# Forgetting attention by pairs of heads with the values as the stationary operand; the mLSTM output gates projected last

## The chip, the cores and the metric

One core of one Trainium2 chip runs the whole program. The metric is the device time of one execution in microseconds (us), and a kernel's time is the median over its runs. The engines are called as in the profile: PE is TensorE's matmuls and PEld its weight loads, DVE is VectorE, ACT is ScalarE, POOL is GpSimd, SP is the queue that issues most DMAs.

## What is computed

Two transformer blocks on 512 tokens of width 1024. The change touches only the mixer of the second block. There 16 meta tokens are put ahead of the 512 (528 rows in all), and two mixers run on the same normalized input: an mLSTM with 4 heads of 128, and a forgetting attention with 8 heads of 64. Cut to what matters:

```python
# mLSTM, per head: h is the stabilised chunk recurrence
h = _rmsnorm(h, out_gain)
h = h * jax.nn.sigmoid(o_pre)
# forgetting attention, per block of 128 queries
logits = einsum('bhtd,bhsd->bhts', qh[:, :, start:end], kh[:, :, :end]) * scale
logits = logits + c[:, :, start:end, None] - c[:, :, None, :end]
logits = where(mask, logits, -inf)
p = softmax(logits)
outs.append(einsum('bhts,bhsd->bhtd', p, vh[:, :, :end]))
# both halves side by side through one output matrix
h_res = h_res + concatenate([y_m, y_f]) @ w_out
```

`o_pre` is a projection of the input (512 columns), `c` the running sum of the forget gates. Later the block ends with a product-key expert layer, which the change leaves alone.

## The kernel before, in words

The program runs through stages: a (gated delta net), b (windowed attention), m (this mixer), p (expert layer). All large projections are made of three fp32r matmuls each (`mm3`, L315 to L317: high by high, high by low, low by high part), accumulated in a PSUM tile `pj`, of which there are two. Weight panels come by `Feed` (line 368): DMA into `wraw`, cast to `whi` on ACT (L233), remainder `wlo` on POOL (L235); six panels are held, in the fixed order of the list that `stage_m` (line 929) hands it, and a panel's place is free when the last step that uses it is done.

In stage m the joint stretch begins where `stage_m` opens the pools `smb` and `pm` (line 1006). Two lists of small steps are built there, each step with a weight, and `weave` (line 334) sorts them into one order by their cumulative weights, so that both lists advance evenly. Within that, a scheduler of the language orders each engine's instructions; an engine then takes them strictly in that order.

- The list `cell` is the mLSTM: first the output-gate projection (16 steps; tanh of it goes into `so`, L1007), then head by head the query and key projections with a convolution (`proj`, taps on DVE in L1195), the weights `mS` (L1216 to L1224, product `pS` on PE), the outputs `pn` (L1232) and, at a head's last tile, the multiplication of the gate and of the norm into `so` (L1246, L1247). Head h+1's projections lie between head h's weights and outputs. For the last head nothing lies there. Then come `mix_turn` (transposes of `so` by PE, `ptz`, L1052) and the first half of the output projection (`mix_out`).
- The list `attend` is the forgetting attention (`fox`): 8 heads, each with 4 query tiles, 32 in all. A tile has three steps. `products`: decay row minus column on DVE (L1281), mask on POOL (L1282), the logits on PE in two matmuls, one for the 16 meta keys (`fo`, L1286) and one for the rest (`pl`, L1287), their minimum with the sum on DVE (L1288, L1289), exponent on ACT (L1290). `turn`: transposes of the probabilities (L1295, L1297) and copies into `fPT`. `values`: one matmul per key tile, with the transposed probabilities as stationary operand (128 columns) and 64 columns of `FV` moving (L1305). At a head's end DVE scales by the reciprocal sums into `yf` (L1308). Before the second half of `mix_out`, `yf` is transposed by PE too.

An ordinary fp32 matmul shows in the trace as two MATMUL and two LDWEIGHTS records; a transpose and an fp32r matmul show as one.

## Time and profile before

| | |
|---|---|
| time, median of 3 runs | 2846.97 us (2841.19 to 2852.54) |
| the profiled execution's own time | 2848.16 us |
| its span, first to last instruction | 2846.4 us |
| mean granted TensorE clock | 0.978 of full |
| PE busy | 2718.2 us (95%) |
| DVE busy | 1973.7 us (69%) |
| ACT busy | 1126.0 us (40%) |
| POOL busy | 836.2 us (29%) |
| the joint stretch of stage m | from about 1235 us to 1484 us, then 23 us of output projection |

How to read it: PE is close to always busy, but busy time counts overlapping matmuls and says nothing of how fast each one went. The clock column (PEclk) tells which of its two levels, 1.2 and 2.4 GHz, PE was granted: 1.00 is 2.4 GHz all through a window, 0.50 is 1.2 GHz all through. The chain of waits says what released each piece of work that the end depended on.

### The profile page before, as it was taken

How to read it: one execution, taken by the hardware profiler on the slowest of the kernel's cores; microseconds unless marked ns; L12 is line 12 of the kernel's file. 1: busy time of each engine (PE TensorE's matmuls, PEld its weight loads, DVE VectorE, ACT ScalarE, POOL GpSimd, SP SyncE). 2: the span in 40 equal slices, each digit the busy share in tenths (PEclk: the TensorE clock that was granted, in tenths of full speed). 3: DMA queues.
4: the chain of work that ended last, by engine and by line, in shares of the span. 5: the costliest groups of instructions: out<-in, count | busy, mean ns of one | idle time of the engine just before them, and what ended most of it. 6: DMA issues, size and time to landing. Idle time of an engine off the chain costs nothing.

```text
span 2846.4 us, 39369 instructions
## 1 busy us (share of the span) xinstructions
PE 2718.2 (95%) x14291; PEld 2250.7 (79%) x14291; DVE 1973.7 (69%) x4339; ACT 1126.0 (40%) x2300; POOL 836.2 (29%) x609
## 2 busy tenths in 40 slices
PE   7999999989999999899998979999999999999999
PEld 5777777767676777677777879899888888888887
DVE  6566666665565645726646899996777877878787
ACT  5444444444444433334322245564333333333332
POOL 0100000000111132232102237774444444444441
PEclk9999999999999999999889989999999999999999
DMA  4112121111222122221103234557999899998996
GB/s 149 53 52 60 60 60 60 53 60 60 75 60 75 62 66 61 63 60 45 31 23 112 87 119 176 177 197 271 308 326 331 316 334 324 318 317 317 319 326 236
DMA packets 170462, 440.92 MB, mean 155 GB/s; under 512 B 13932, under 2 KB 79756, under 8 KB 168604
## 3 DMA queue, kind: packets, MB, share of 16 engines
q1 hardware_dynamic: 133404, 304.17, 33.0%
q0 software_dynamic: 36864, 134.23, 12.5%
q8 instruction: 113, 1.85, 0.3%
q14 instruction: 81, 0.66, 0.1%
HBM read 401.60 MB, written 36.75 MB: 154 GB/s over the span
## 4 chain that ended last, share of the span: by engine, by line
PE 66%; DVE 16%; issue 7%; ACT 5%; DMA 3%; POOL 3%; SPq 0%; ACTq 0%; DVEq 0%; POOLq 0%
PE pj L315 11%; PE pj L316 11%; PE pj L317 10%; PE acc L316 4%; PE acc L317 4%; PE acc L315 3%; PE pG L1611 2%; ACT whio L233 2%; DVE x L1479 2%; DMA raw<-in_v_dram 2%; PE po L922 1%; DVE wloo L235 1%; PE fo L1305 1%; PE po L316 1%; PE po L315 1%
## 5 line engine op out<-in xcount | busy, mean ns | idle before, releaser
L315 PE MATMUL pj<-hThi,whi 128*128 128x384 f32 (+2 forms) x1664 | 603.4, 363 | 2.7 <-ACT hg L1357 2.1
L317 PE MATMUL pj<-hThi,wlo 128*128 128x384 f32 (+2 forms) x1664 | 593.5, 357 | 10.9 <-DVE wlo L235 10.9
L316 PE MATMUL pj<-hTlo,whi 128*128 128x384 f32 (+2 forms) x1664 | 597.4, 359 | 0.2 <-DVE hTlo L213 0.2
L317 PEld LDWEIGHTS pj<-hThi,wlo 128*128 128x128 f32 x1664 | 316.6, 190 | 32.1 <-DVE wlo L235 11.5
L315 PEld LDWEIGHTS pj<-hThi,whi 128*128 128x128 f32 x1664 | 317.1, 191 | 31.1 <-ACT hg L1357 2.7
L316 PEld LDWEIGHTS pj<-hTlo,whi 128*128 128x128 f32 x1664 | 316.8, 190 | 24.8 <-DVE hTlo L213 1.2
L316 PE MATMUL acc<-wloo,Wh 128*128 128x512 f32 x768 | 303.1, 395 | 5.8 <-DVE wloo L235 4.4
L315 PE MATMUL acc<-whio,Wh 128*128 128x512 f32 x768 | 301.2, 392 | 0.8 <-ACT whio L233 0.8
L317 PE MATMUL acc<-whio,Wl 128*128 128x512 f32 x768 | 300.2, 391 | 0.0
L1470 POOL DMA_INDIRECT raw<-in_v_dram,ids x128 | 191.7, 1498 | 238.1 <-DVE wloo L235 120.9
L1470 POOL DMA_INDIRECT raw<-in_u_dram,ids x128 | 185.9, 1452 | 242.6 <-DVE wloo L235 110.9
L212 ACT CAST Wh<-W 128x384 fp32r<-128x384 f32 x128 | 65.7, 513 | 372.9 <-DVE W L1417 337.7
L235 DVE TENSOR_TENSOR wlo<-raw,whi 128x1024 fp32r<-128x1024 f32 x128 | 161.7, 1263 | 71.7 <-ACT whi L233 71.6
L233 ACT CAST whi<-raw 128x1024 fp32r<-128x1024 f32 x144 | 150.2, 1043 | 124.2 <-issue 92.7
L235 DVE TENSOR_TENSOR wloo<-raw,whio 128x1024 fp32r<-128x1024 f32 x128 | 156.9, 1226 | 53.7 <-ACT whio L233 53.7
L316 PEld LDWEIGHTS acc<-wloo,Wh 128*128 128x128 f32 x768 | 144.2, 188 | 46.1 <-DVE wloo L235 18.5
L235 POOL TENSOR_TENSOR wlo<-wraw,whi 128x1024 fp32r<-128x1024 f32 x52 | 124.4, 2406 | 187.3 <-ACT whi L233 187.1
L317 PEld LDWEIGHTS acc<-whio,Wl 128*128 128x128 f32 x768 | 144.2, 188 | 30.5
L315 PEld LDWEIGHTS acc<-whio,Wh 128*128 128x128 f32 x768 | 144.1, 188 | 30.4 <-ACT whio L233 2.4
L1479 DVE SCALAR_TENSOR_TENSOR x<-raw,act,x 128x1024 f32<-128x1024 f32 x128 | 163.8, 1280 | 1.0
L1474 DVE SCALAR_TENSOR_TENSOR raw<-raw,xt 128x1024 f32<-128x1024 f32 x128 | 154.0, 1219 | 0.0
L233 ACT CAST whi<-wraw 128x1024 fp32r<-128x1024 f32 x100 | 104.4, 1047 | 107.0 <-PE pj L316 68.3
(418 smaller groups left out, 5483.4 us busy)
## 6 DMA issues: line engine op xcount, KB each, us to landing
raw<-in_uT_dram SPq DMA_DIRECT2D x128, 512.0 KB, 4.6
raw<-in_v_dram SPq DMA_DIRECT2D x128, 512.0 KB, 5.1
wraw<-in_wa_dram SPq DMA_DIRECT2D x48, 512.0 KB, 3.6
G<-stage SPq DMA_DIRECT2D x12, 2048.0 KB
Gt<-G SPq DMA_DIRECT2D x32, 768.0 KB, 10.3
wraw<-in_wb_dram SPq DMA_DIRECT2D x32, 512.0 KB, 3.8
wraw<-in_wmt_dram SPq DMA_DIRECT2D x20, 512.0 KB, 3.6
H<-hg SPq DMA_DIRECT2D x48, 192.0 KB, 1.9
```

The lines of the kernel that those rows point to most:

```text
L212: self.nc.scalar.copy(hi, src)
L233: nc.scalar.copy(hi, raw)
L235: eng.tensor_tensor(out=lo, in0=raw, in1=hi.bitcast(F32), op=ALU.subtract)
L315: nc.tensor.matmul(out, wh, mh, start=first, stop=False)
L316: nc.tensor.matmul(out, wh, ml, start=False, stop=False)
L317: nc.tensor.matmul(out, wl, mh, start=False, stop=last)
L922: nc.tensor.matmul(po[:, (4 * b + h) * 64 : (4 * b + h + 1) * 64], PT[:, h * nst + st, :], V[:, s0 // P + st, g * 64 : (g + 1) * 64], star ...
L1305: nc.tensor.matmul(d["o"][:, 64 * t : 64 * t + 64], u["PT"][0:n, j, :], FV[0:n, j, h * 64 : (h + 1) * 64], start=(j == 0), stop=(j == t + 1))
L1470: nc.gpsimd.indirect_dma_start(out=g, out_offset=None, in_=src, in_offset=bass.IndirectOffsetOnAxis(ap=ids[:, j : j + 1], axis=0))
L1474: nc.vector.scalar_tensor_tensor(g, g, 1.0, xt0, op0=ALU.mult, op1=ALU.mult, accum_out=act[:, j : j + 1])
L1479: nc.vector.scalar_tensor_tensor(k.x[:, 0, :], g, act[:, j : j + 1], k.x[:, 0, :], op0=ALU.mult, op1=ALU.add)
L1611: nc.tensor.matmul(p[:, n * P : (n + 1) * P], o1[:, n, :], o0[:, n, :], start=True, stop=True)
```

## The change

The attention goes by pairs of heads. A query tile of a pair is one unit (16 in all): both heads' `products`, both heads' `turn`, and one `values`, in which the 64 columns of `FV` are the stationary operand and the transposed probabilities (128 columns) move; head 0 of the pair writes PSUM partitions 0 to 63, head 1 partitions 64 to 127, alternating key tile by key tile. The result is already transposed, so `mix_turn` for `yf` is replaced by `mix_split`, which makes the high and low parts without PE. The division by the sums now runs along partitions: eight matmuls per pair (`pr`) spread the reciprocal sums over the array, ACT copies them, DVE multiplies. The 16 meta keys have no matmul of their own any more for the first three tiles (one product of 144, 272 or 400 columns); only the last, with 528 columns, keeps two. `fo` has one buffer in place of two, and a bank `fm` takes the small pieces.

The output gates of the mLSTM are projected last: eight of the sixteen steps lie between the weights and outputs of head 3, where nothing lay; the other eight follow head 3. `so` holds the normalized outputs first, and `use_gate` multiplies (1 + tanh) in. The first two gate tiles stay in the two `pj` buffers until head 3 is done. The four gate panels move in the feed from ahead of the eight query/key panels to behind them. (V1 is also padded from 130 to 132 columns; the matmul still reads 130.)

```diff
@@ -929,11 +929,11 @@
-    feed = Feed(k, [(a["wmt"][4 * i + c], None) for i in (4, 3, 2, 0, 1) for c in range(4)] + [(a["wmc"][i], None) for i in range(8)]
-                + [(a["wmo"][4 * c + 2 * h + j], None) for h in range(2) for c in range(2) for j in range(2)], 6)
+    feed = Feed(k, [(a["wmt"][4 * i + c], None) for i in (4, 3, 2, 0) for c in range(4)] + [(a["wmc"][i], None) for i in range(8)]
+                + [(a["wmt"][4 + c], None) for c in range(4)] + [(a["wmo"][4 * c + 2 * h + j], None) for h in range(2) for c in range(2) for j in range(2)], 6)
-        yf = s3.tile([P, NT, 512], F32, name="yf")
+        yf = s3.tile([P, 4, T], F32, name="yf")
...
@@ -1004,13 +1004,22 @@
-                cell = tproj(4, range(1, 5), lambda j, n, p: nc.scalar.activation(so[:, j - 1, :], p, AF.Tanh, scale=0.5))
+                held = []
+
+                def use_gate(j, p):
+
+                    th = s2.tile([P, T], F32, tag="mM", name="th")
+                    nc.scalar.activation(th, p, AF.Tanh, scale=0.5)
+                    nc.vector.scalar_tensor_tensor(so[:, j - 1, :], th, 1.0, so[:, j - 1, :], op0=ALU.add, op1=ALU.mult)
+
+                gate = tproj(6, range(1, 5), lambda j, n, p: held.append(p) if j < 3 else use_gate(j, p))
                 heads = [mlstm(k, s2, h, hh, hl, V1, colR, rowM, so, feed) for h in range(4)]
-                cell += heads[0][0][0] + heads[0][0][1]
+                cell = heads[0][0][0] + heads[0][0][1]
                 for h in range(4):
                     (p0, p1), run, w, o = heads[h]
-                    n0, n1 = heads[h + 1][0] if h < 3 else ([], [])
+                    n0, n1 = heads[h + 1][0] if h < 3 else (gate[0:4], gate[4:8])
                     cell += [run] + n0 + w[0:2] + n1 + [w[2], o[0], w[3], o[1], w[4], o[2], o[3]]
+                cell += [(0.1, lambda j=j: use_gate(j, held[j - 1])) for j in (1, 2)] + gate[8:]
...
@@ -1020,21 +1029,22 @@
-                heads = [fox(k, s2, h, fqT, fkT, FV, colC, rowC, yf) for h in range(8)]
-                tiles = [t for _, l in heads for t in l]
-                turns = mix_turn(k, yf, 4, out)
-                attend.append(heads[0][0])
-                for i, (pr, tr, mu) in enumerate(tiles):
+                pairs = [fox(k, s2, c, fqT, fkT, FV, colC, rowC, yf) for c in range(4)]
+                units = [u for _, l in pairs for u in l]
+                turns = mix_split(k, yf, 4, out)
+                attend += pairs[0][0]
+                for i, (pr, tr, _) in enumerate(units):
+                    for j in range(2):
+                        if i:
+                            attend.append(units[i - 1][1][j])
+                        attend.append(pr[j])
+                        if i % 4 == 3 and i < 15:
+                            attend.append(pairs[i // 4 + 1][0][j])
                     if i:
-                        attend.append(tiles[i - 1][1])
-                    attend.append(pr)
-                    if i:
-                        attend.append(tiles[i - 1][2])
-                    if i % 4 == 2 and i // 4 < 7:
-                        attend.append(heads[i // 4 + 1][0])
-                    if i in (28, 29, 30):
-                        attend.append(turns[i - 28])
-                attend += tiles[-1][1:]
+                        attend.append(units[i - 1][2])
+                    if i in (13, 14, 15):
+                        attend.append(turns[i - 13])
+                attend += units[-1][1] + [units[-1][2]]
...
+
+def mix_split(k, y, k0, out):
+
+    def step(kt):
+        yh, yl = out()
+        k.split(yh[:, kt, 0:T], yl[:, kt, 0:T], y[:, kt - k0, :])
+
+    return [(0.1, lambda kt=kt: step(kt)) for kt in range(k0, k0 + 4)]
...
     def proj(j):
-        ct, i0 = 4 * j + h, 20 + 2 * h + j
+        ct, i0 = 4 * j + h, 16 + 2 * h + j
...
@@ -1243,74 +1262,88 @@
         if t == NT - 1:
             r = k.rnorm(d["ss"], 128.0, NT)
             sh = so[:, :, h * P : (h + 1) * P]
-            nc.vector.scalar_tensor_tensor(sh, sh, 1.0, y, op0=ALU.add, op1=ALU.mult)
-            nc.vector.tensor_tensor(out=sh, in0=sh, in1=r.rearrange("p (n o) -> p n o", o=1).to_broadcast([P, NT, P]), op=ALU.mult)
+            nc.vector.tensor_tensor(out=sh, in0=y, in1=r.rearrange("p (n o) -> p n o", o=1).to_broadcast([P, NT, P]), op=ALU.mult)
...
-def fox(k, s2, h, fqT, fkT, FV, colC, C, yf):
-    ct, js = h // 2, slice(64 * (h % 2), 64 * (h % 2) + 64)
     d = {}
+    half = [slice(0, 64), slice(64, P)]
+
+    def gates(j):
...
     def parts(t):
-        u = {}
-
-        def products():
-            if t == 0:
-
-                d["o"] = k.pm.tile([P, 512], F32, tag="fo", name="fo", bufs=2)
-                d["sum"] = k.sm.tile([P, NT], F32, tag="fsm", name="fsm")
-            dB = s2.tile([P, TM], F32, tag="dB", name="dB", bufs=3)
...
+        lg, PT = {}, {}
+        ts = slice(t * P, (t + 1) * P)
+
+        def products(j):
+            h, js = 2 * c + j, half[j]
+            if t == j == 0:
+
+                d["o"] = k.pm.tile([P, 512], F32, tag="fo", name="fo", bufs=1)
+                d["m"] = k.pm.tile([P, 512], F32, tag="fm", name="fm", bufs=1)
+                d["sum"] = k.sm.tile([P, 2, NT], F32, tag="fsm", name="fsm")
+            lg[j] = dB = s2.tile([P, TM], F32, tag="dB", name="dB", bufs=3)
...
-            m = k.sm.tile([P, 2], F32, tag="fm", name="fm")
+            m = k.sm.tile([P, 2], F32, tag="fmm", name="fmm")
             p = ps("pl")
-            qt = fqT[js, ct, t * P : (t + 1) * P]
-            nc.tensor.matmul(pm, qt, fkT[js, ct, 0:16], start=True, stop=True)
-            nc.tensor.matmul(p[:, 0 : W - 16], qt, fkT[js, ct, 16:W], start=True, stop=True)
-            nc.vector.tensor_tensor_reduce(dB[:, 0:16], pm, dB[:, 0:16], 1.0, -NEG, ALU.add, ALU.min, m[:, 0:1])
-            nc.vector.tensor_tensor_reduce(dB[:, 16:W], p[:, 0 : W - 16], dB[:, 16:W], 1.0, m[:, 0:1], ALU.add, ALU.min, m[:, 1:2])
-            nc.scalar.activation(dB[:, 0:W], dB[:, 0:W], AF.Exp, scale=-1.0, bias=m[:, 1:2], accum_out=d["sum"][:, t : t + 1])
-            u["lg"] = dB
-
-        def turn():
-            pt, pmT, lg = ps("pt"), d["o"][0:16, 320:448], u["lg"]
-            nc.tensor.transpose(pmT, lg[:, 0:16], k.ident)
-            for j in range(t + 1):
-                nc.tensor.transpose(pt[:, j * P : (j + 1) * P], lg[:, 16 + j * P : 16 + (j + 1) * P], k.ident)
-            u["PT"] = PT = s2.tile([P, 5, P], F32, tag="fPT", name="fPT", bufs=2)
-            nc.scalar.copy(PT[0:16, 0, :], pmT)
-            nc.vector.tensor_copy(PT[:, 1 : t + 2, :], pt[:, 0 : (t + 1) * P].rearrange("p (j c) -> p j c", c=P))
+            qt = fqT[js, c, ts]
+            if W > 512:
+                pm = d["m"][:, 16 * j : 16 * j + 16]
+                nc.tensor.matmul(pm, qt, fkT[js, c, 0:16], start=True, stop=True)
+                nc.tensor.matmul(p[:, 0 : W - 16], qt, fkT[js, c, 16:W], start=True, stop=True)
+                nc.vector.tensor_tensor_reduce(dB[:, 0:16], pm, dB[:, 0:16], 1.0, -NEG, ALU.add, ALU.min, m[:, 0:1])
+                nc.vector.tensor_tensor_reduce(dB[:, 16:W], p[:, 0 : W - 16], dB[:, 16:W], 1.0, m[:, 0:1], ALU.add, ALU.min, m[:, 1:2])
+            else:
+                nc.tensor.matmul(p[:, 0:W], qt, fkT[js, c, 0:W], start=True, stop=True)
+                nc.vector.tensor_tensor_reduce(dB[:, 0:W], p[:, 0:W], dB[:, 0:W], 1.0, -NEG, ALU.add, ALU.min, m[:, 1:2])
+            nc.scalar.activation(dB[:, 0:W], dB[:, 0:W], AF.Exp, scale=-1.0, bias=m[:, 1:2], accum_out=d["sum"][:, j, t : t + 1])
+
+        def turn(j):
+            pt, o = ps("pt"), 128 + P * ((2 * t + j) % 3)
+            pmT = d["m"][0:16, o : o + P]
+            nc.tensor.transpose(pmT, lg[j][:, 0:16], k.ident)
+            for i in range(t + 1):
+                nc.tensor.transpose(pt[:, i * P : (i + 1) * P], lg[j][:, 16 + i * P : 16 + (i + 1) * P], k.ident)
+            PT[j] = s2.tile([P, 5, P], F32, tag="fPT", name="fPT", bufs=2)
+            nc.scalar.copy(PT[j][0:16, 0, :], pmT)
+            nc.vector.tensor_copy(PT[j][:, 1 : t + 2, :], pt[:, 0 : (t + 1) * P].rearrange("p (j c) -> p j c", c=P))
...
         def values():
-            for j in range(t + 2):
-                n = ST[j][1]
-                nc.tensor.matmul(d["o"][:, 64 * t : 64 * t + 64], u["PT"][0:n, j, :], FV[0:n, j, h * 64 : (h + 1) * 64], start=(j == 0), stop=(j == t + 1))
+            for i in range(t + 2):
+                n = ST[i][1]
+                for j in range(2):
+                    h = 2 * c + j
+                    nc.tensor.matmul(d["o"][half[j], ts], FV[0:n, i, h * 64 : (h + 1) * 64], PT[j][0:n, i, :], start=(i == 0), stop=(i == t + 1))
             if t == NT - 1:
+
                 nc.vector.reciprocal(d["sum"], d["sum"])
-                nc.vector.tensor_tensor(out=yf[:, :, h * 64 : (h + 1) * 64], in0=d["o"][:, 0:256].rearrange("p (n c) -> p n c", n=NT),
-                                        in1=d["sum"].rearrange("p (n o) -> p n o", o=1).to_broadcast([P, NT, 64]), op=ALU.mult)
-
-        return [(0.4 + 0.2 * t, products), (0.11 * (t + 2), turn), (0.11 * (t + 2), values)]
-
-    return (0.5, gates), [parts(t) for t in range(NT)]
+                p = ps("pr")
+                for n in range(NT):
+                    for j in range(2):
+                        nc.tensor.matmul(p[half[j], n * P : (n + 1) * P], d["sum"][:, j, n : n + 1].to_broadcast([P, 64]), k.ident, start=True, stop=True)
+                nc.scalar.copy(yf[:, c, :], p)
+                nc.vector.tensor_tensor(out=yf[:, c, :], in0=d["o"], in1=yf[:, c, :], op=ALU.mult)
+        two = lambda w, f: [(w, lambda j=j: f(j)) for j in range(2)]
+        return two(0.4 + 0.2 * t, products), two(0.11 * (t + 2), turn), (0.15 * (t + 2), values)
+
+    return [(0.5, lambda j=j: gates(j)) for j in range(2)], [parts(t) for t in range(NT)]
```

What moves on PE, at the last head of the mLSTM (`pS` its weights, `pn` its outputs, `fo`, `fm`, `pt`, `pl` the attention's pieces). Before:

```order
L1295 MATMUL fo<-cst,dB 16x128
L1223 MATMUL pS<-mqk_11962,mqk_12092 16x512
L1223 MATMUL pS<-mqk_11962,mqk_12092 128x512
L1297 MATMUL pt<-cst,dB 128x128 x3
L1287 MATMUL pl<-fkT,fqT 128x512
L1223 MATMUL pS<-mqk_11962,mqk_12092 128x384
L1232 MATMUL pn<-V_9564,mS_12324 128x130
L1232 MATMUL pn<-V_9564,mS_12339 128x130
L1286 MATMUL fo<-fkT,fqT 128x16
L1305 MATMUL fo<-FV,fPT 128x64 x4
```

and in the changed kernel at the same place:

```order
L315 MATMUL pj<-whi,hThi 128x512
L316 MATMUL pj<-wlo,hThi 128x512
L317 MATMUL pj<-whi,hTlo 128x512
L1242 MATMUL pS<-mqk_11659,mqk_11786 128x384
L1332 MATMUL fo<-fPT,FV 64x128 x8
L1251 MATMUL pn<-V_9564,mS_12084 128x130
L1251 MATMUL pn<-V_9564,mS_12090 128x130
```

Before, some 50 rows of PE around this place hold no projection (`pj`) at all; now triples of the gate projection stand between them, six matmuls at a time.

On PE, where a head's third tile gives its values, before (the last two rows are the next head's first products):

```order
L1305 MATMUL fo<-FV,fPT 128x64 x4
L1295 MATMUL fo<-cst,dB 16x128
L1297 MATMUL pt<-cst,dB 128x128 x4
L1286 MATMUL fo<-fkT,fqT 128x16
L1287 MATMUL pl<-fkT,fqT 128x128
```

and in the changed kernel, the second tile's values of the first pair (6 matmuls for two heads; the first of them stands ahead of the projections before this place):

```order
L1313 MATMUL pl<-fkT,fqT 128x400
L1332 MATMUL fo<-fPT,FV 64x128 x5
L1320 MATMUL fm<-cst,dB 16x128
L1322 MATMUL pt<-cst,dB 128x128 x3
L1308 MATMUL fm<-fkT,fqT 128x16
```

The values of two heads stand in one burst, with 64 stationary columns and 128 moving; the 16-column product is left only before the 512-column one. With the tiles' numbers shown, the matmuls of a burst alternate between the two heads' `fPT` all through the 16 units.

## Rows read from the trace of the kernel before

**Rows 1.** The page, part 1: busy us (share of the span) and instructions of each engine.
```profile
PE 2718.2 (95%) x14291; PEld 2250.7 (79%) x14291; DVE 1973.7 (69%) x4339; ACT 1126.0 (40%) x2300; POOL 836.2 (29%) x609
```

**Rows 2.** Windows of the joint stretch: length, busy us (count) PE PEld DVE ACT POOL, PEclk, DMA, GB/s.
```profile
1234.70:1400.00 165.30, 162.47 (x933) 124.93 (x932) 89.43 (x304) 64.19 (x161) 45.64 (x40) 0.96 0.17 49
...
1407.60:1449.00 41.40, 40.79 (x130) 28.22 (x131) 20.87 (x85) 11.15 (x38) 1.32 (x3) 0.51 0.00 1
```

**Rows 3.** Windows of 20 us, same columns, before 1400 us, in which PEclk is under 1.
```profile
1240.00:1260.00 20.00, 19.53 (x81) 12.85 (x80) 8.57 (x24) 5.39 (x14) 6.94 (x8) 0.91 0.17 52
...
1320.00:1340.00 20.00, 19.85 (x102) 15.10 (x100) 10.10 (x38) 5.62 (x19) 3.27 (x3) 0.83 0.09 27
...
1380.00:1400.00 20.00, 20.00 (x118) 15.74 (x119) 13.19 (x50) 8.61 (x22) 3.97 (x4) 0.91 0.09 27
```

**Rows 4.** Waits of the matmul engine in that stage: us in total, times, longest.
```profile
PE pn L1232 <- DVE mS L1224: 2.9, 1, 2.9
```

**Rows 5.** Groups by line and shape there: xcount | busy us, mean ns | idle.
```profile
L1305 PE MATMUL fo<-FV,fPT 128*128 128x64 f32 x160 | 26.8, 302 | 0.0
...
L1305 PE MATMUL fo<-FV,fPT 16*128 16x64 f32 x64 | 14.9, 316 | 0.7 <-DVE fm L1288 0.7
L1286 PE MATMUL fo<-fkT,fqT 64*128 64x16 f32 x64 | 11.7, 268 | 0.0
```

**Rows 6.** Timeline of PE: start us, busy us; two bursts of values and the next instruction.
```profile
1246.16 0.80 PE L1305 MATMUL fo<-FV,fPT 16*128 16x64 f32 x4 [0.40 <-DVE fm L1288]
1246.77 0.48 PE L316 MATMUL pj<-wlo,hThi 128*128 128x512 f32 x1
...
1267.56 1.47 PE L1305 MATMUL fo<-FV,fPT 16*128 16x64 f32 x10
1268.87 0.27 PE L1295 MATMUL fo<-cst,dB 128*16 128x128 f32 x1
```

**Rows 7.** Timeline of PE, first stage: eight records in alternating column halves (L654).
```profile
73.96 0.45 PE L654 MATMUL pp<-X,LTc 128*64 128x64 f32 x8
74.35 0.50 PE L316 MATMUL pj<-hTlo,whi 128*128 128x512 f32 x1
```

**Rows 8.** Timeline of PE, first stage: eight records in one column half (L676).
```profile
93.89 0.68 PE L676 MATMUL py<-Y,Pm 128*64 128x64 f32 x8
94.50 0.50 PE L315 MATMUL pj<-hThi,whi 128*128 128x512 f32 x1
```

**Rows 9.** Timeline of PE: the 16-column product and the wide one behind it.
```profile
1321.76 0.39 PE L1286 MATMUL fo<-fkT,fqT 64*128 64x16 f32 x2
1322.01 0.68 PE L1287 MATMUL pl<-fkT,fqT 64*128 64x256 f32 x2
```

**Rows 10.** Chain that ended last: start us, length us, what; wide products, a burst of transposes.
```profile
1322.15 0.53 PE pl L1287 x2
...
1458.80 0.44 PE ptz L1052 x4
1468.48 0.95 PE pl L1287 x2
```

**Rows 11.** Chain that ended last, around 1407 us.
```profile
1404.69 2.40 DVE mqk L1195 x6
...
1413.69 5.08 PE pn L1232 x18
1418.78 1.66 PE fo L1305 x6
```

**Rows 12.** Chain that ended last, the same pieces at the upper clock.
```profile
1359.28 0.95 PE fo L1305 x6
...
1374.46 2.79 PE pn L1232 x18
```

**Rows 13.** Tile so: duration ns min/median/max, first and last start us.
```profile
L1007 ACT ACTIVATE so<-pj x4: 586/598/598, 1248.2 to 1279.0; 128x512 f32<-128x512 f32 x4
L1246 DVE SCALAR_TENSOR_TENSOR so<-so,my x4: 682/688/693, 1342.8 to 1448.1; 128x512 f32<-128x512 f32 x4
```

More of the change, by code (lines that the diff above doesn't have):

```diff
@@ L944, in stage_m @@
             fkT = s1.tile([P, 4, TM], F32, name="fkT")
-            V1 = s1.tile([P, 5, 4, 130], F32, name="V1")
+            V1 = s1.tile([P, 5, 4, 132], F32, name="V1")
             nc.gpsimd.memset(V1[:, :, :, 128:129], 1.0)
@@ L1231, in outputs @@
             S, t0 = d["S"][j]
-            nc.tensor.matmul(pn[:, 0:130], S[0:n, t * P - t0 : t * P - t0 + P], V1[0:n, j, h, :], start=(j == 0), stop=(j == t + 1))
+            nc.tensor.matmul(pn[:, 0:130], S[0:n, t * P - t0 : t * P - t0 + P], V1[0:n, j, h, 0:130], start=(j == 0), stop=(j == t + 1))
         q = k.sm.tile([P, 1], F32, tag="md", name="md")
@@ L1251, in mlstm, with fox @@
             [(0.25 * t + 0.5, lambda t=t: outputs(t)) for t in range(NT)])
-def fox(k, s2, h, fqT, fkT, FV, colC, C, yf):
+def fox(k, s2, c, fqT, fkT, FV, colC, C, yf):
     nc = k.nc
-    ct, js = h // 2, slice(64 * (h % 2), 64 * (h % 2) + 64)
     d = {}
     ps = lambda name: k.pm.tile([P, 512], F32, tag="fx", name=name, bufs=2)
-    def gates():
-        d["c"] = s2.tile([P, TM], F32, tag="ncB", name="ncB", bufs=2)
+    half = [slice(0, 64), slice(64, P)]
+    def gates(j):
+        d[j] = s2.tile([P, TM], F32, tag="ncB", name="ncB", bufs=2)
         for i in range(2):
@@ L1265, in gates @@
             pc = ps("pc")
-            k.spread(pc[:, 0:264], [r[:, sl] for r in C], h, 32)
-            nc.scalar.copy(d["c"][:, sl], pc[:, 0:264])
+            k.spread(pc[:, 0:264], [r[:, sl] for r in C], 2 * c + j, 32)
+            nc.scalar.copy(d[j][:, sl], pc[:, 0:264])
     def parts(t):
         W = 16 + P * (t + 1)
-        u = {}
-        def products():
-            if t == 0:
-                d["o"] = k.pm.tile([P, 512], F32, tag="fo", name="fo", bufs=2)
-                d["sum"] = k.sm.tile([P, NT], F32, tag="fsm", name="fsm")
-            pm = d["o"][:, 256 + 16 * t : 272 + 16 * t]
-            dB = s2.tile([P, TM], F32, tag="dB", name="dB", bufs=3)
-            nc.vector.tensor_scalar(out=dB[:, 0:W], in0=d["c"][:, 0:W], scalar1=colC[:, t + 1, h : h + 1], scalar2=None, op0=ALU.subtract)
+        lg, PT = {}, {}
@@ new lines, in parts @@
+        ts = slice(t * P, (t + 1) * P)
[6 more added lines that the diff above has]
+            lg[j] = dB = s2.tile([P, TM], F32, tag="dB", name="dB", bufs=3)
+            nc.vector.tensor_scalar(out=dB[:, 0:W], in0=d[j][:, 0:W], scalar1=colC[:, t + 1, h : h + 1], scalar2=None, op0=ALU.subtract)
```

## The prediction

> **What bounds the kernel now.** I read the page first: PE is busy 95% of the span [rows 1], so time is gained only where PE gets less work, runs it faster or waits less. Then I cut the joint stretch of mLSTM and attention into windows. From 1234.7 to 1400 us PE is busy 162.5 of 165.3 us at a mean clock of 0.96; no other engine is near its limit, DVE with 89.4 us (54%) comes next. From 1407.6 to 1449 us PE is busy 40.8 of 41.4 us, but at a clock of 0.51 [rows 2]: the lower of the two levels nearly throughout. Three windows before it hold short dips [rows 3]. Of PE's waits only one is long: 2.9 us for a weight tile from DVE [rows 4], at 1404.7 to 1407.6 us, while DVE worked off six taps in 2.4 us [rows 11]. The clock fell at the end of that wait and did not rise for 41 us. What PE did in that time is known from the order: no projection, only small fp32 pieces. So the stretch has two prices: PE's work at full clock, and a tail in which the same work goes at half speed.
>
> **Values.** 224 records stand for 112 fp32 matmuls [rows 5]. A burst of two takes 0.61 us from its start to the next instruction (1246.16 to 1246.77), one of five 1.31 us (1267.56 to 1268.87) [rows 6], so a key tile costs (1.31 - 0.61) / 3 = 0.233 us and a burst 0.14 us of start. A head (2, 3, 4 and 5 key tiles) takes 3.8 us, eight heads 30.6 us. In the changed kernel a matmul has half as many stationary columns and twice as many moving ones, and two stand in different column halves. Whether the halves overlap is read from the first stage. Eight records that alternate between the halves take 0.45 us [rows 7], eight in one half 0.68 us [rows 8]; the last record alone lasts some 0.22 us, so first to last start is 0.23 us against 0.46 us: half. If that holds with 128 moving columns, two heads' key tile costs what one head's does now, a pair takes 3.8 us and four pairs 15.3 us: **15 us less**. The bounds are 15.3 us (full overlap) and nothing (none). I take 15 because the rows with alternating halves are the same kind of matmul.
>
> Each burst now also switches the array's shape. The rows price it: the 0.14 us of start above contains such a switch, since a burst opens with a 16-row matmul. The Trainium skill (TensorEngine Tiling (Array Packing), Key Properties) says that a change of tiling mode drains the engine. Charged once more for 16 bursts and 4 spreads, at the row's 0.14 us, that would take 2.8 us of the gain away; no run here shows whether the narrower tiles drain longer. Those 2.8 us lie inside the forecast's own range.
>
> **The 16-column products.** The product for the meta keys goes in 24 of 32 tiles. It takes 0.25 us to the start of the next [rows 9], so 6.0 us less; its columns join the wide product, whose two sizes in the chain (0.53 us at 256 columns, 0.95 us at 512) [rows 10] give 1.6 ns a column, 24 x 16 x 1.6 ns = 0.6 us more. The Trainium skill (the same page, Instruction Overhead) counts some 60 cycles for a matmul with few columns. By that, 24 products of two records at 2.4 GHz would be worth 1.2 us, and the saving 4.8 us smaller; the row shows 0.25 us, and the row decides. DVE loses 24 minima; it is not the bound, so nothing is counted.
>
> **Spread and transposes.** Eight new matmuls per pair spread the reciprocal sums. Each pair of them costs like a key tile, 4 x 0.233 + 0.14 = 1.07 us, four times 4.3 us (8.0 us without overlap). The four bursts of transposes of `yf` go: 4 x 0.44 = 1.8 us less [rows 10]. The ACT copies and DVE multiplications of the spread lie beside PE's work, except at the last pair, where the second half of the output projection covers them with its first matmuls.
>
> At full clock this is -15.3 - 6.0 + 0.6 + 4.3 - 1.8 = **-18 us** on PE.
>
> **The gates last.** The 96 matmuls of the gate projection move with four casts on ACT, four subtractions on POOL and four DMAs; the panels now follow the eight query/key panels in the queue, and POOL, ACT and the DMA engines are far from full where they land (1.3 us, 11.2 us and a share of 0.00 in 41.4 us) [rows 2]. So the move adds no work; it puts dense projections into the tail. The same pieces show what that is worth: 18 output records take 5.08 us in the tail and 2.79 us before it, six of values 1.66 against 0.95 us [rows 11, 12], a factor of 1.8. At the upper level the tail's 41.4 us would be 23.0: 18.4 us less, with the wait of 2.9 us at most 21.3 us. The lower bound is zero, if the clock falls elsewhere instead. I take two thirds, **-14 us**: before, the clock also dipped where projections stood between the pieces, at 1240, 1320 and 1380 us [rows 3], so some of this comes back. What is late next: the transposes of `so` now wait for the last gate tile, tanh on ACT (0.59 us) and a multiplication on DVE (about 0.69 us, as the one it replaces) [rows 13]; with the hand-over 1.5 us, and little cover is left. The first two gate tiles hold both `pj` buffers until head 3 is done, and no other projection is due then. **+1.5 us.**
>
> **The sum.** -18 - 14 + 1.5 = -30.5 us. The profiled execution took 2848.2 us (span 2846.4 and 1.8 around it), so 2817.7; the median of the runs stands 1.2 us lower: **2816.5 us**. The expert stage behind starts after the mixer and should shift as a whole.
>
> **Rivals.**
> 1. *The column halves don't overlap at 128 moving columns.* For it: the pair of rows is from 64 moving columns. Against: the halving there is exact. Values then save nothing and the spread costs 8.0 us: -6.0 + 0.6 + 8.0 - 1.8 = +0.8 on PE; -14 + 1.5 more gives -11.7, or 2835 us.
> 2. *The slow tail moves forward.* Denser pieces at the ends of heads 0 to 2 lower the clock there for as long. For it: the dips at 1320 and 1380 us [rows 3] stand at such head ends. Against: they were over within 7 us (6.8 and 3.6 us of low clock). -18 + 1.5 = -16.5, or 2830.5 us.
> 3. *Slower: the clock falls early in the stretch and stays down.* The values now come in 16 bursts on half the columns, and if those no longer keep the clock up, the low level lasts. Low time before: 3.6 + 6.8 + 3.6 us in the three windows [rows 3] and 40.6 us in the tail [rows 2], 55 us in all. At 1.8 a low microsecond costs 0.44 us. With 150 us low: (150 - 55) x 0.44 = 42, less 16.5: +25, or 2872 us. It turns slower than before by 14 us at (16.5 + 14) / 0.44 + 55 = 124 us of low clock. Against: the projections between are the same in number.
>
> That the change doesn't do what it says is excluded as far as the order goes: the two heads' matmuls alternate.
>
> **How the numbers follow.** Forecast 0.66, no overlap 0.09, tail moved 0.19, slower 0.06. About 0.5% (14 us) is what a measurement of this kernel can tell from no change. The forecast lies 30 us below the old median and is faster almost surely (0.65 of 0.66); the moved tail at -16.5 is in 0.11 of 0.19; no overlap at -12 in 0.03 of 0.09. Faster 0.79, same 0.16, slower 0.05. The forecast's own bounds are -18 - 21.3 (2809) with some dips gone too, and the rivals 1 and 2 reach 2835; taking the lower edge for the three dips at 14 x 0.44 = 6 us: range **2803 to 2835 us**.
>
> **What would show it.** The line of values with 64x128 tiles should take some 3.8 us a pair, a burst of ten 1.3 us. The joint stretch should be some 30 us shorter. The clock column should be 1.00 where head 3 ends, and low windows should sum to 20 us or so. The 16-column line should have 16 records. The prediction is wrong if a burst of ten takes over 2 us (rival 1), if a row of windows at 0.5 stands somewhere else (2, 3), or if PE shows a new wait of several us: for `fo`, which has one buffer now, or for the gates ahead of the transposes.

## The result, and the profile after

The changed kernel takes **2818.9 us** (median of 4 runs, 2814.33 to 2819.4); the kernel before, timed beside it, 2844.08 us (2839.55 to 2852.54). The ratio on record is 0.9888, with a 95% interval of 0.9859 to 0.9917: faster by 0.8 to 1.4% (the two medians by themselves give 0.9911, inside that interval). The forecast was 2816.5 us. The profiled execution took 2819.12 us, with a span of 2817.4 us and a clock of 0.984.

The page of the changed kernel, part 1, answers to [rows 1]: PE is 31.6 us less busy, at the same 95%.

```profile
PE 2686.6 (95%) x14291; PEld 2219.0 (79%) x14291; DVE 1966.2 (70%) x4283; ACT 1128.3 (40%) x2304; POOL 839.0 (30%) x609
```

From here on "the stretch" runs from the first spread of a gate row (`pc`) to the first instruction of the expert stage (`xt`). It took 260.1 us before (1235.7 to 1495.8) and takes 232.3 now (1236.5 to 1468.8), 27.8 us less; it starts 0.8 us later, and what is behind it is 2.0 us shorter. So 27.8 of the 29.0 us are here. Its windows in the changed kernel (length, busy us and count of PE, PEld, DVE, ACT, POOL, PEclk, DMA share, GB/s):

```profile
1236.50:1468.80 232.30, 224.87 (x1309) 162.95 (x1309) 131.64 (x403) 89.80 (x226) 56.54 (x49) 0.96 0.14 44
1240.00:1260.00 20.00, 18.15 (x81) 14.02 (x82) 12.73 (x31) 9.24 (x23) 11.63 (x9) 0.71 0.27 83
1320.00:1340.00 20.00, 19.74 (x122) 14.66 (x122) 11.25 (x41) 7.88 (x24) 3.48 (x3) 1.00 0.07 27
1380.00:1400.00 20.00, 20.00 (x114) 13.97 (x112) 9.18 (x35) 5.04 (x19) 1.37 (x3) 1.00 0.00 1
1400.00:1449.00 49.00, 45.69 (x271) 32.09 (x268) 25.23 (x58) 17.03 (x38) 12.48 (x9) 0.97 0.14 44
```

The tail, at 0.51 over 41.4 us before [rows 2], now has 0.97 (1400 to 1449 us). Head 3's pieces, which stood in it from 1422 to 1446 us, now stand from 1378 to 1399 us, at 1.00. The dips at 1320 and 1380 us [rows 3] are gone here; the one at 1240 us has grown, from 0.91 to 0.71. Summed over the clock's records, the lower level lasts 17.1 us in the stretch, 54.6 before.

Groups of PE by line and shape in the stretch (xcount | busy us, mean ns | idle before, releaser). They answer to [rows 5]; L1339 is the new spread of the reciprocal sums:

```profile
L1332 PE MATMUL fo<-fPT,FV 128*64 128x128 f32 x160 | 13.8, 284 | 0.0
L1332 PE MATMUL fo<-fPT,FV 16*64 16x128 f32 x64 | 10.4, 294 | 0.6 <-ACT fPT L1324 0.6
L1339 PE MATMUL pr<-cst,fsm 128*64 128x128 f32 x64 | 5.8, 277 | 0.0
L1308 PE MATMUL fm<-fkT,fqT 64*128 64x16 f32 x16 | 3.1, 270 | 0.0
```

The chain that ended last (start us, length us, what). It answers to [rows 11, 12]. The 18 output records of [rows 11] are those of head 2, whose end the old tail held too; head 3's own, before:

```profile
1441.32 5.09 PE pn L1232 x18
```

In the changed kernel head 3's last 18 come in two pieces, 1.28 and 1.50 us, with projections between. Whole bursts of four, eight and ten values (8, 16 and 20 records) take 0.73, 1.17 and 1.39 us:

```profile
1267.48 0.95 PE fo L1332 x10
1269.37 0.36 PE fo L1332 x2
...
1288.79 1.16 PE fo L1332 x14
...
1321.64 0.59 PE fo L1332 x8
...
1389.66 1.17 PE fo L1332 x16
...
1395.59 1.28 PE pn L1251 x8
...
1397.33 1.50 PE pn L1251 x10
...
1399.77 1.39 PE fo L1332 x20
1401.16 0.87 PE pr L1339 x16
...
1409.95 0.73 PE fo L1332 x8
```

PE's waits in the stretch (total, times, longest); the wait of [rows 4] is gone, and a longer one stands at the tail's end:

```profile
PE ptz L1062 <- DVE so L1013: 3.3, 1, 3.3
PE pc L278 <- ACT ncB L1285: 2.2, 1, 2.2
PE pj L315 <- DVE mqk L1214: 0.7, 1, 0.7
```

**Where the time went.** I summed PE's records in the stretch from each start to the next, with the waits by themselves, and divided those at the lower level by 1.8, the factor of [rows 11, 12]. That parts the work from the clock.

| term | before | after | difference | predicted |
|---|---|---|---|---|
| values | 30.1 | 20.1 | -10.0 | -15.3 |
| 16-column products, wide products | 8.0 + 22.6 | 2.2 + 24.0 | -4.4 | -5.4 |
| spread `pr` | 0 | 5.1 | +5.1 | +4.3 |
| transposes `ptz` | 3.6 | 2.1 | -1.5 | -1.8 |
| waits, all else | 172.0 | 171.9 | -0.1 | +1.5 |
| **work** | | | **-10.9** | **-16.7** |
| lost at the lower level | 23.8 | 7.0 | **-16.8** | **-14** |

The prediction's -14 holds the old wait of 2.9 us too; here that is among the waits.

### The profile page after: what moved, and what is told of

The parts are those of the page before. It is cut to its first block, busy times and chain, and to the rows that moved or that the text cites. A ratio compares the mean times of both kernels' runs of the same rounds, so it can differ in the third digit from the quotient of the medians.

```text
span 2817.4 us, 39316 instructions
## 1 busy us (share of the span) xinstructions
PE 2686.6 (95%) x14291; PEld 2219.0 (79%) x14291; DVE 1966.2 (70%) x4283; ACT 1128.3 (40%) x2304; POOL 839.0 (30%) x609
## 4 chain that ended last, share of the span: by engine, by line
PE 68%; DVE 16%; issue 6%; ACT 5%; POOL 3%; DMA 2%; SPq 0%; ACTq 0%; DVEq 0%; POOLq 0%
PE pj L315 11%; PE pj L316 11%; PE pj L317 11%; PE acc L316 4%; PE acc L317 4%; PE acc L315 4%; ACT whio L233 2%; PE po L922 2%; PE pG L1644 1%; DVE x L1512 1%; DVE wloo L235 1%; DVE wlo L235 1%; PE po L316 1%; POOL o L1634 1%; PE po L315 1%
## 5 line engine op out<-in xcount | busy, mean ns | idle before, releaser
L317 PEld LDWEIGHTS pj<-hThi,wlo 128*128 128x128 f32 x1664 | 317.4, 191 | 33.9 <-DVE wlo L235 12.5
L1503 POOL DMA_INDIRECT raw<-in_u_dram,ids x128 | 185.5, 1449 | 243.7 <-DVE wloo L235 115.0
```

The lines of the kernel that those rows point to most:

```text
L317: nc.tensor.matmul(out, wl, mh, start=False, stop=last)
L1503: nc.gpsimd.indirect_dma_start(out=g, out_offset=None, in_=src, in_offset=bass.IndirectOffsetOnAxis(ap=ids[:, j : j + 1], axis=0))
```

## The experiments

Every run below is compared with the kernel before on its own chip, whose median was 2853.0 us for the first four, 2854.2 for the next four and 2851.3 for the last four. Executions differ by several us with the clock, so the stretch of each profile is shown with it. "At the upper level" is the stretch less 0.44 us for each us at the lower, the prediction's price. The last column is the mean granted clock over all executions timed (their number), which a single profile can't give.

| kernel | ratio to before (95%) | stretch | low in it | at the upper level | clock |
|---|---|---|---|---|---|
| before | 1 | 260.1 | 54.6 | 236.1 | 0.976 (45) |
| changed | 0.9888 (0.9859 to 0.9917) | 232.3 | 17.1 | 224.8 | 0.985 (4) |
| changed, again | 0.9911 (0.9879 to 0.9943) | 242.2 | 41.0 | 224.2 | 0.982 (4) |
| gates last only | 0.9943 (0.9920 to 0.9966) | 249.0 | 30.7 | 235.5 | 0.981 (8) |
| pairs only | 0.9912 (0.9877 to 0.9946) | 235.0 | 20.5 | 226.0 | 0.983 (4) |
| halves apart | 0.9931 (0.9907 to 0.9955) | 244.8 | 20.5 | 235.8 | 0.983 (6) |
| meta keys apart | 0.9958 (0.9938 to 0.9978) | 247.3 | 34.1 | 232.3 | 0.979 (10) |
| gates behind head 3 | 0.9884 (0.9850 to 0.9917) | 233.4 | 20.5 | 224.4 | 0.983 (4) |
| pairs only, meta keys apart | 0.9986 (0.9971 to 1.0000) | 262.9 | 64.9 | 234.3 | 0.977 (10) |
| meta keys joined only | 0.9977 (0.9960 to 0.9994) | 259.8 | 68.3 | 229.7 | 0.976 (10) |
| first spread on DVE | 0.9889 (0.9855 to 0.9923) | 228.4 | 13.7 | 222.4 | 0.983 (4) |
| first spread on DVE, again | 0.9897 (0.9865 to 0.9930) | 229.7 | 17.1 | 222.2 | 0.983 (4) |
| tanh in PSUM | 0.9885 (0.9850 to 0.9921) | 239.7 | 30.7 | 226.2 | 0.984 (4) |
| both of these | 0.9872 (0.9836 to 0.9907) | 231.8 | 17.1 | 224.3 | 0.984 (4) |

### The changed kernel again

> The changed kernel once more, on the chip of the next run, to see how far its joint stretch and its low clock repeat. Expected: the stretch 229 to 236 us (232.3 in its first profile), low clock in it 14 to 24 us, and a ratio to before of 0.986 to 0.992.

The ratio is 0.9911, inside the range, the stretch 242.2 us and outside it. At the upper level it repeats to 0.6 us; the low clock doesn't, 41.0 us in place of 17.1. Half of it is one piece at head 1's end, which this window takes in:

```profile
1326.00:1352.00 26.00, 25.74 (x113) 19.94 (x113) 11.99 (x52) 8.85 (x26) 1.44 (x3) 0.61 0.05 20
```

So work is read from one profile to about a microsecond, and the clock only from many executions.

### Gates last only

The kernel before, with the feed's order, `use_gate` and the step lists of the change; `fox` by single heads as before.

> Single heads as before, only the gate projection last. Theory (the pairs and the gate order gain independently): 14 us less low clock and wait in the tail, 1.5 us more for the transposes of so, so about 12 us below the kernel before, 2832 us, and no window of low clock longer than 7 us near head 3's end. Rival (the clock in the tail came back because the pairs are shorter, not because projections stand there): 2844 us, the slow tail of some 40 us still there.

2836.5 us against 2853.0, 16 us less. At the upper level the stretch is the same as before (235.5 to 236.1), and low clock falls from 54.6 to 30.7 us. Windows of the stretch and of its tail:

```profile
1235.70:1484.70 249.00, 243.45 (x1309) 187.04 (x1309) 137.10 (x459) 87.56 (x222) 54.35 (x50) 0.94 0.13 41
1400.00:1449.00 49.00, 47.76 (x239) 35.05 (x238) 26.93 (x85) 17.56 (x44) 12.22 (x10) 0.93 0.15 44
```

The tail is up. By itself the move does what the theory said, and somewhat more.

### Pairs only

The changed kernel with the gate projection first again (the feed's order, tanh into `so`, the multiplication at a head's last tile, as before).

> Pairs of heads, the gate projection first as before. Theory: PE has 18 us less to do, so 2826 us, and the slow tail is there again: some 35 to 41 us of low clock where head 3 ends, pn x18 at 5 us. Rival (the pairs alone bring the clock back): 2814 to 2819 us without the slow tail. Second rival (the column halves give nothing and all the gain is the gate order's): 2844 us.

2825.3 us against 2853.0: 28 us less, not 18, so the first rival came true. The window of this kernel's tail:

```profile
1400.00:1449.00 49.00, 46.35 (x241) 30.81 (x238) 32.61 (x116) 16.23 (x49) 4.34 (x7) 0.97 0.02 7
```

and head 3's last 24 output records in the chain (the first six stand in a short low piece of 3.4 us):

```profile
1419.00 1.82 PE pn L1242 x6
...
1422.84 1.28 PE pn L1242 x8
...
1424.49 1.50 PE pn L1242 x10
```

No projection stands between head 3's pieces here. On PE's timeline the last one before them and the next one are 33 us apart:

```profile
1394.08 0.29 PE L317 MATMUL pj<-hThi,wlo 128*128 128x264 f32 x1
...
1427.59 0.50 PE L315 MATMUL pj<-whi,hThi 128*128 128x512 f32 x1
```

In the kernel before, 48 us passed without a projection (1401.0 to 1448.8), 41.0 of them at the lower level; here it is 3.4 of 33, and the window's clock is 0.97. The whole stretch is 2.7 us longer than the changed kernel's 232.3, and the ratios, 0.9912 and 0.9888 to 0.9911, can't be told apart. So with the pairs there, the gates' place is worth little or nothing.

### Halves apart

```diff
-            for i in range(t + 2):
-                n = ST[i][1]
-                for j in range(2):
+            for j in range(2):
+                for i in range(t + 2):
```

(the same in the loops of `pr`)

> The changed kernel with the same matmuls, but all of one column half before the other in each burst of values and in the spread of the reciprocal sums. Theory (neighbours in different halves overlap): a burst of ten takes 0.14 + 10 x 0.233 = 2.5 us in place of 1.4, the pairs 4 x 7.1 = 28 us in place of 15 and the spread some 3 us more, so 14 to 16 us above the changed kernel, 2834 us. Rival (64 stationary columns are quick by themselves, the alternation does nothing): 2819 us and a burst of ten at 1.4 us.

The stretch is 12.5 us longer than the changed kernel's, 11.0 of it at the upper level; 14 to 16 were expected. The chain shows whole bursts of eight matmuls (16 records) at 2.31 us, where the changed kernel has 1.17:

```profile
1398.30 2.31 PE fo L1332 x16
...
1454.02 2.31 PE fo L1332 x16
```

The overlap of the column halves is real and nearly complete; narrow tiles alone give nothing.

### Meta keys apart

```diff
-            if W > 512:
+            if True:
```

> The changed kernel with the 16-column product by itself in all 32 tiles again, as before the change. Theory (its price is the 0.25 us of its row, less what the 16 columns take in the wide product): 24 x 0.25 - 0.6 = 5.4 us above the changed kernel, 2824 us. Rival (most of the 0.25 us is start-up of the burst that the wide product then pays, or such a product costs 1.2 us in all): 0 to 1 us above, 2819 to 2820 us.

More than the theory: the ratio is 0.9958 against 0.9888 and 0.9911 of the changed kernel. At the upper level 232.3 against 224.2 to 224.8 is 7.5 to 8.1 us. The rest is clock: 0.979 over ten executions, none above 0.983, and 17 us of low clock in one piece at 1332 us.

### Gates behind head 3

In the list, all 16 steps of the gate projection stand behind head 3, so that none should lie between its pieces.

```diff
-                    n0, n1 = heads[h + 1][0] if h < 3 else (gate[0:4], gate[4:8])
+                    n0, n1 = heads[h + 1][0] if h < 3 else ([], [])
...
-                cell += [...] + gate[8:]
+                cell += gate[0:8] + [...] + gate[8:]
```

> The changed kernel with all 16 steps of the gate projection behind head 3; none stand between head 3's pieces. Theory (dense projections keep the clock up only where they stand between the small pieces): head 3's pieces fall to the lower level, 15 to 25 us of low clock, 7 to 11 us above the changed kernel, 2826 to 2830 us. Rival (what brought the clock back is the lost wait of 2.9 us or the shorter tail, not the filling): 2819 us, no low window at head 3.

The time is the rival's: 2821.0 us, a stretch of 233.4 us, 0.93 in the window from 1400 to 1449 us (6.8 us low), no slow stretch. But the trace shows that the edit didn't take the filling away, because the scheduler drew projections forward again. Of the 96 matmuls of the gate projection 7 stand ahead of head 3's first weights (24 in the changed kernel) and 16 between its pieces (26). PE's timeline at head 3's last outputs:

```profile
1386.58 1.35 PE L1251 MATMUL pn<-V,mS 16*128 16x130 f32 x8
1387.68 0.48 PE L316 MATMUL pj<-wlo,hThi 128*128 128x512 f32 x1
1388.09 1.57 PE L1251 MATMUL pn<-V,mS 16*128 16x130 f32 x10
1389.42 0.48 PE L317 MATMUL pj<-whi,hTlo 128*128 128x512 f32 x1
```

So this run has less filling, not none, and doesn't decide between theory and rival. The run with the pairs alone does: there the clock stays up without any filling.

### Which part of the pairs lifts the clock

Two kernels: the pairs alone with the 16-column product apart in all tiles, and the kernel before with nothing but that product joined.

> Pairs only (gates first), and the 16-column product by itself in all 32 tiles. Theory A (what lifted the clock at head 3 in the run with the pairs alone was that the 16-column products are gone): the slow tail is there again, 25 to 41 us of low clock where head 3 ends, the joint stretch 5 us of work and 10 to 18 us of clock longer than with the pairs alone, 250 to 258 us. Theory B (the values on column halves lifted it, whatever the 16-column products do): 5 us longer, 240 us, and no low window over 7 us at head 3.

> The kernel before, with one edit: the 16 meta keys' columns joined to the wide product in 24 of 32 tiles. Theory A (these products also held the clock down): 5.4 us of work less and the slow tail gone, so the joint stretch 19 to 23 us shorter than the 260 us of before, 237 to 241 us. Theory B (only the pairs' values or the filling with projections lift it): 5 us shorter, 255 us, the slow tail of some 40 us still there.

Windows around head 3's end, first of the pairs with the products apart:

```profile
1407.00:1460.00 53.00, 48.65 (x210) 32.30 (x208) 33.74 (x124) 17.09 (x51) 5.40 (x7) 0.74 0.03 11
```

and of the kernel before with them joined:

```profile
1410.00:1455.00 45.00, 42.57 (x150) 27.94 (x149) 25.49 (x94) 13.03 (x42) 3.88 (x5) 0.62 0.04 13
```

The pairs with the products apart have a slow tail again and 64.9 us of low clock: theory A for this kernel. But joining them alone saves its 6.4 us of work and lifts nothing (68.3 us): theory B for that one. So, with the gates first, the pairs (their values, spread, missing transposes and order, which no run takes apart) and the joined products lift the clock only together. Without the joining the pairs gain almost nothing: 2846.8 us against 2851.3.

### The wait at the start of the stretch

In the changed kernel PE waits there 2.2 us for `ncB`: ACT stands at a cast whose panel is still on its way, and the copies that PE needs are queued behind it. ACT's timeline (start us, busy us, in brackets the idle time before):

```profile
1239.43 1.04 ACT L233 CAST whi<-wraw 128x1024 fp32r<-128x1024 f32 x1 [2.94 <-DMA wraw<-in_wmc_dram]
1240.38 0.65 ACT L1285 COPY ncB<-pc 128x264 f32<-128x264 f32 x2
```

```diff
-            nc.scalar.copy(d[j][:, sl], pc[:, 0:264])
+            (nc.scalar.copy if c else nc.vector.tensor_copy)(d[j][:, sl], pc[:, 0:264])
```

> The changed kernel with the first pair's four copies of the spread gate row (ncB) on DVE; on ACT they stand behind a cast that waits 2.9 us for a panel's DMA. Theory: PE's wait of 2.2 us for pc goes, and with it the low clock behind it (6.8 us, 3 us of time): 2 to 5 us less, 2814 to 2817 us. Rival (PE then waits for the next thing, the panel itself): 0 to 1 us less.

> The first spread's copies on DVE once more, beside the changed kernel on the same chip. Theory (the wait of 2.2 us and the clock that it cost are gone every time): the joint stretch 3 to 4 us shorter than the changed kernel's, the median 2 to 5 us lower. Rival (the first difference of 3.9 us was the scatter of the clock): medians within 1.5 us of each other.

The wait is gone in both profiles, and low clock in the first 25 us of the stretch falls from 13.7 us (in both profiles of the changed kernel) to 3.4 and 6.8; a shorter wait is next. PE's waits in the second:

```profile
PE ptz L1062 <- DVE so L1013: 3.2, 1, 3.2
PE fm L1320 <- ACT dB L1315: 1.3, 1, 1.3
```

At the upper level the stretch is 222.4 and 222.2 us, against 224.8 and 224.2 of the changed kernel: 2 us, twice. On the same chip the medians are 2821.0 and 2824.6 us; the intervals overlap, so whether that is a gain in time stays open.

### The wait for the last gate tile

```diff
-                    th = s2.tile([P, T], F32, tag="mM", name="th")
-                    nc.scalar.activation(th, p, AF.Tanh, scale=0.5)
-                    nc.vector.scalar_tensor_tensor(so[:, j - 1, :], th, 1.0, so[:, j - 1, :], op0=ALU.add, op1=ALU.mult)
+                    nc.scalar.activation(p, p, AF.Tanh, scale=0.5)
+                    nc.vector.scalar_tensor_tensor(so[:, j - 1, :], p, 1.0, so[:, j - 1, :], op0=ALU.add, op1=ALU.mult)
```

> The changed kernel with the gates' tanh written back into its PSUM tile, so that the multiplication into so has one operand in PSUM and one in SBUF, not two in SBUF. Theory (with two SBUF operands DVE stands still until POOL's subtraction beside it is over): the last multiplication takes 0.6 to 0.8 us in place of 2.44, PE's wait of 3.3 us for so becomes 1.5 us, the time 2 to 3 us less with the dip behind it, 2816 to 2817 us. Rival (POOL and DVE share something that every DVE instruction meets): it still takes 2.4 us, 2819 us.

The multiplication takes 0.68 us and PE's wait is 1.5 us, as expected; the time isn't less. Of the two subtractions for `yf` on DVE, the one that came beside POOL now took 1.81 us, and PE waits 1.4 us more for `hThi`. DVE, and below it POOL, in this run:

```profile
1425.21 1.81 DVE L213 TENSOR_TENSOR hTlo<-yf,hThi 128x512 fp32r<-128x512 f32 x1 [4.69 <-ACT hThi L212]
1426.94 0.68 DVE L1012 SCALAR_TENSOR_TENSOR so<-pj,so 128x512 f32<-128x512 f32 x1
1427.54 0.67 DVE L213 TENSOR_TENSOR hTlo<-yf,hThi 128x512 fp32r<-128x512 f32 x1
...
1421.73 4.74 POOL L235 TENSOR_TENSOR wlo<-wraw,whi 128x1024 fp32r<-128x1024 f32 x2 [9.09 <-ACT whi L233]
```

POOL is done at 1426.47, the slow subtraction at 1427.02. The hold-up moved to another instruction with two SBUF operands. The edit also changed PE's order: for 20 us (1391.6 to 1411.8) no projection stands there, where the changed kernel has at most 8 us without one, so the run's time holds more than the wait. No POOL work ran beside the new multiplication, so the run doesn't show directly that the PSUM operand frees it.

### Both of these

> Both edits, the first spread's copies on DVE and tanh in PSUM. Theory: they add up, 4 to 7 us less than the changed kernel, 2812 to 2815 us. Rival (the low clock moves on to other places): 0 to 2 us less.

The ratio, 0.9872, is the lowest here, and its interval holds those of the changed kernel. At the upper level 224.3 us is no better than the changed kernel: the edit at the tail seems to take back what the one at the start gives. A version that is surely faster than the changed kernel wasn't found.

## Why the prediction was right, point by point

- **Values.** Mechanism right, size off: -10.0 us, not -15.3. The step that failed is "a pair takes 3.8 us"; it took 5.0. Two things are in this. First, whole bursts of two, four and five pairs of matmuls take 0.73, 1.17 and 1.39 us: 0.22 us for a pair of neighbours and 0.29 us of start, where 0.233 and 0.14 were counted. With whole bursts alone the values would have taken 17.0 us, 1.7 more than in the sum. Second, the sum counts 16 whole bursts, and they stand in 27 pieces, many cut after the first matmul, with other work, mostly projections, between. Pieces of 0.36 and 0.95 us make 1.31 where a whole burst of six takes 0.95; 0.36 and 1.16 make 1.52 where one of eight takes 1.17. The 11 cuts took the other 3.1 us, some 0.3 us each. The last order excerpt ahead of the prediction showed such a cut. Before, 32 bursts stood in 39 pieces, and the burst time of [rows 6] was right for them. Halves apart, a burst of eight takes 2.31 us.
- **Switching the array's shape.** The prediction weighed 2.8 us for it and left it out of the sum. It shows: the start of a burst is 0.15 us longer than the 0.14 counted, 2.4 us for 16 whole bursts. A piece that opens with 128 rows and not with 16 shows 0.15 us of start by itself (four matmuls 0.59 us). Where the shape doesn't change there is none: the spread behind the burst of ten takes 0.87 us for eight matmuls, four times 0.22. The Trainium skill (TensorEngine Tiling (Array Packing), Key Properties) says that a change of tiling mode drains the engine. The trace agrees in so far as the start comes with the change of shape; the rows don't tell a drain from anything else in it.
- **16-column products.** -5.8 us for the products themselves, -6.0 predicted; the wide ones cost 1.4 us more, not 0.6. Joined alone they save 6.0 us and the wide ones cost 1.5 more; the stretch at the upper level is 6.4 us shorter. The row of 0.25 us was the right price, for work. That they also weigh on the clock wasn't in the sum.
- **Spread and transposes.** +5.1 and -1.5 us against +4.3 and -1.8.
- **The gates last, -14 us.** The clock did give 16.8 us in this profile, but the step "it puts dense projections into the tail" isn't what is shown to have done it. The move alone does lift the tail (low clock 30.7 us in place of 54.6). But with the gates first the pairs have it at 0.97 too, through 33 us without a projection. For the tail either suffices, and they don't add: 11.1 us of stretch for the gates alone, 25.1 for the pairs alone, 27.8 and, in the second profile, 17.9 for both; the mean clocks are 0.981, 0.983 and, for both, 0.985 and 0.982. So the prediction was right in its total, with the work's gain 5.8 us too large, the clock term 2.8 us too small, and the clock put down to one cause of two. That the total came so close is in part luck, since the two errors have opposite signs and the clock scatters: in the second profile of the changed kernel the lower level costs 17.2 us, only 6.6 less than before. An estimate from all executions is steadier: 0.983 over 8 against 0.976 over 45 is some 40 us less at the lower level in the whole program, 18 us at 0.44 us each. That the 2.9 us wait [rows 4] started the old fall isn't shown, and such a wait isn't needed: in the kernel with the products joined only, the clock fell at 1415 us with no wait over 0.6 us near it.
- **The wait for `so`, +1.5 us.** It is 3.3 us, a new wait of the kind that the prediction had named among its signs of being wrong. The hand-over was foreseen, not that the last multiplication takes 2.44 us in place of 0.69 (below).
- **Rivals.** No overlap: excluded by the halves apart. The slow tail that moves forward came true in part: in the second profile of the changed kernel, 20.5 us of low clock stand at 1329 us, where the prediction had put that rival, and low clock sums to 41.0 us. So the figure of 20 us holds for some executions, not for all. Slower, by a clock that falls early and stays: not seen.

What stays open is what in the small pieces holds the clock down. No single edit explains all the runs: joined products lift it with pairs (0.977 to 0.983) and not with single heads (0.976 both times).

## What to carry to other kernels

Two matmuls with 64 stationary columns each, neighbours in different column halves, take the time of one (a burst of eight 1.17 us, against 2.31 one half after the other); keep a burst together, since each cut costs more than another such pair (some 0.3 us against 0.22). When a stretch runs at the lower clock, price work and clock apart, and undo the parts one at a time: several edits can each restore the clock, and their gains don't add. A move that only fills a gap is worth its own run before it is given the credit, and the trace of that run has to be read for whether the gap was really filled or emptied: the order of a list isn't yet the order on the engine.

## What the runs showed of the hardware that was not expected

**DVE stands still beside POOL.** The last gate multiplication, with both tensors in SBUF, took 2.44 us where three others took 0.68 to 0.98 us. In the changed kernel's timeline (start us, busy us; first DVE, then POOL):

```profile
1418.77 2.44 DVE L1013 SCALAR_TENSOR_TENSOR so<-th,so 128x512 f32<-128x512 f32 x1 [0.42 <-ACT th L1012]
...
1418.32 2.34 POOL L235 TENSOR_TENSOR wlo<-wraw,whi 128x1024 fp32r<-128x1024 f32 x1 [1.94 <-ACT whi L233]
```

POOL started first and ended at 1420.66; DVE ended 0.55 us later, at 1421.21, as if it had begun only then. At the start of the stretch the same happened to a decay row (2.29 us, ended 0.23 us after POOL), while a DVE instruction with one operand in PSUM ran in 0.31 us beside POOL, as it did with POOL idle (at 1248.86 us). The same timeline, first DVE, then POOL:

```profile
1245.34 0.31 DVE L1314 CUSTOM_DVE_ANT_0 dB<-pl,dB 128x144 f32<-128x144 f32 x1 [1.64 <-PE pl L1313]
...
1248.86 0.31 DVE L1314 CUSTOM_DVE_ANT_0 dB<-pl,dB 128x144 f32<-128x144 f32 x1 [3.21 <-PE pl L1313]
...
1251.86 2.29 DVE L1301 TENSOR_SCALAR dB<-ncB,colC 128x400 f32<-128x400 f32 x1
...
1243.50 2.42 POOL L235 TENSOR_TENSOR wlo<-wraw,whi 128x1024 fp32r<-128x1024 f32 x1
...
1251.57 2.35 POOL L235 TENSOR_TENSOR wlo<-wraw,whi 128x1024 fp32r<-128x1024 f32 x1 [1.32 <-ACT whi L233]
...
1257.65 2.73 POOL L1302 TENSOR_TENSOR dB<-dB,cst 128x128 f32<-128x128 f32 x1 [2.90 <-DVE dB L1301]
```

It goes the other way too: the last line is a mask that takes POOL 0.46 us elsewhere; here DVE had begun first, at 1257.50 us, on a row of such instructions, and the mask took 2.73 us.

The Trainium skill (SBUF — State Buffer, Who interferes with whom) says why: a DVE instruction with two SBUF inputs, or in a two-port mode, shares a port with POOL, and whoever starts first holds it for the whole instruction. The trace agrees in each of these cases. So "the multiplication it replaces took 0.69 us" [rows 13] held only as long as POOL was quiet beside it.
